# Sparse attention's first part laid out anew: keys by pairs of tiles, an order written out by hand, search steps spread differently

## The chip, the cores and the metric

The kernel runs on one core of one Trainium2 chip. The metric is device microseconds of one launch, taken as the median of several runs. Five engines work beside each other, each with its own queue of instructions: PE (TensorE, matmuls and transposes), DVE (VectorE), ACT (ScalarE), POOL (GpSimd) and SP, which here only issues transfers. An engine works through its queue strictly in order. PEld, where it appears, is the loading of weights on PE.

## The reference, cut to what matters

The program computes a two-layer decoder trunk on 1024 rows of 1024 numbers, in float32: sparse attention, a dense part, a gated recurrence and a second dense part. The change touches the attention alone, and of it what comes ahead of the softmax. In the reference that is:

```
h = x @ w_in
c_q, k, v, k_idx, w_idx = jnp.split(h, [256, 384, 512, 640], axis=-1)
c_q = rms_norm(c_q, g_cq)
q = (c_q @ w_uq)          # 16 heads of 64
q_idx = (c_q @ w_iq)      # 8 index heads of 128
k_idx = layer_norm(k_idx, g_ik, b_ik)
q, k, q_idx, k_idx = rope of each
score = einsum(w_idx, relu(q_idx . k_idx)), causal
_, sel = lax.top_k(score, 256)
out = softmax over the selected keys only, then @ w_o
```

Each query keeps the 256 keys with the highest score. The first 256 rows (tiles 0 and 1 of eight tiles of 128 rows) have no more than 256 causal keys, so they need no score.

## The kernel before, in words

**Tiles.** The rows are worked on as eight tiles of 128. Numbers with full float32 accuracy are made by three products of a high and a low part (`mm3`, lines 103 to 105), so a matmul of the source is three on PE, and `split` or `part` (lines 209, 210, 1186, 1187) makes the two parts, one on ACT and one on DVE.

**The first part, `att_in` (line 1150).** For each tile t there are five steps.
- `feature(t)` (line 1189) turns the tile of x by eight transposes on PE and splits it.
- `project(t)` (line 1214) multiplies it with `w_in`: 48 matmuls, 24 with 384 columns and 24 with 264.
- `keys(t)` (line 1233) makes what later tiles look at: on DVE it takes 33 instructions, among them the reciprocal root `rsqrt` (lines 111 to 116, eleven short instructions in a chain), two applications of `rope` (lines 202 to 205, four each), the norm's scaling (1255 to 1258), copies of keys out of PSUM (1269) and the low parts (1253, 210). PE makes seven transposes.
- `query(t)` (line 1282) makes the queries and the index queries, 12 matmuls of 512 columns each (24 in all), and POOL applies `rope` to both.
- `store(t)` (line 1305) turns them on PE in halves of eight transposes and writes them to DRAM. Of tiles 0 and 1 only the queries are written; their index queries are computed and never read.

**Scores and search.** `index(j)` (line 1356) makes the scores of tile j in units. A unit is three matmuls, a Relu on ACT (1383) and one instruction on DVE that adds the weighted result to the scores (1388). Tiles 2 and 3 have 8 units each, tiles 4 to 7 have 16 each, 80 in all. When the last unit of a tile is done, POOL masks its last 128 columns (1391). `search(js)` (line 1408) then finds the 256th highest score of two tiles at a time, bit by bit: twice 16 steps, each with a count on ACT (1436) for one tile and on DVE (1437) for the other, and two short instructions on DVE (1442, 1444) that set the next bound. With the steps ahead, between and behind it has 48 steps for each of the pairs (2, 3), (4, 5) and (6, 7). It ends with the mask of allowed keys, `bias` (1487).

**The second part, `att_main` (line 1491).** For each tile j there are 16 heads: logits on PE (1688), mask and minimum on DVE (1690), Exp on ACT (1692), transposes (1659), a copy on ACT (1661), products with the values (1664), and every eight heads `heads_out` (1694). The output projection (`att_out`) follows some heads later. Beside the heads of tile 1, POOL makes low parts of `w_o` (1505).

**What sets the order.** The program lists instructions in the order in which the Python code runs, and the framework then gives each engine a fixed queue; an instruction listed later may be put ahead of one that would wait. Scores and search are generators: `advance(i)` takes `STEPS[i]` = (units, steps) of them at four or five points of round i in `att_in`, and `att_main` takes `PLAN[j]` = (units, steps) behind each head of tile j. A generator that has to wait (for a tile that isn't stored, or for a buffer of scores that is still searched) gives its turn back without work. Worked out from these tables, the first part before takes 78 of the 80 units and 62 of the 144 search steps, the heads of tiles 0 and 1 take 2 units and 20 steps, and the heads of tiles 2 to 5 the other 62 steps. Round i of the first part lists `project(i)`, `store(i-2)`, `feature(i+1)`, `query(i-1)` and `keys(i)`:

```
        for i in range(NT + 2):
            if i < NT:
                project(i)
...
            if i >= 2:
                store(i - 2)
            advance(i)
            if i + 1 < NT:
                feature(i + 1)
            if 1 <= i <= NT:
                query(i - 1)
```

Transfers are all issued by SP, in order: the loads of x, the writes of `store` (1318), the loads of index queries (1366) and of queries (1585).

## Time and profile before

| what | value |
|---|---|
| median of 3 runs | 2638.32 us (2635.59 to 2641.08) |
| the profiled execution's own time | 2633.86 us |
| its span | 2632.1 us |
| PE busy | 2515.4 us, 96% |
| DVE busy | 2013.9 us, 77% |
| ACT busy | 1129.7 us, 43% |
| POOL busy | 250.0 us, 9% |
| mean granted clock of TensorE | 0.978 of full speed |

The table is of the whole span, in which attention takes about the first 700 us and the dense parts and the recurrence the rest. A share of busy time over the whole span therefore says little about the stretch that the change touches, and the stretches are read one by one below. Times inside the profile count from the span's start. Matmuls overlap in the pipeline, so the time between two starts is what a matmul costs, not its own length.

### The profile page before, as it was taken

The page shows a single profiled execution, that of the slowest core. Times are in us where ns is not written, and L with a number is a line of the kernel's source. Part 1 is how long each engine was busy: PE and PEld are TensorE (multiplying, and loading weights), DVE is VectorE, ACT ScalarE, POOL GpSimd, SP SyncE. Part 2 cuts the span into 40 slices and gives each one's busy share as a digit, 9 for nine tenths or more (in the row PEclk, how much of TensorE's full clock was granted, in tenths as well). Part 3 has the DMA queues.
Part 4 walks back from the last instruction along what each step waited for, and adds up shares of the span by engine and source line. Part 5 has one row for each costly group of instructions (what it writes and reads, how often), then busy time and mean ns, then how long its engine had stood idle before and what let it go on. Part 6 is the DMA issues. An engine that isn't in the chain of part 4 may idle for free.

```text
span 2632.1 us, 36939 instructions
## 1 busy us (share of the span) xinstructions
PE 2515.4 (96%) x13102; PEld 2090.3 (79%) x13102; DVE 2013.9 (77%) x4042; ACT 1129.7 (43%) x2176; POOL 250.0 (9%) x334
## 2 busy tenths in 40 slices
PE   8976799999999999999999999999899999999998
PEld 7764678888888788878788888888678888888786
DVE  6599899787778776656778888887786887665667
ACT  4576667665533233343544333333344323333431
POOL 1323421210000000000002111111000000000000
PEclk9998799999999999999999999999899999999999
DMA  3213200100366643385531111112535673336853
GB/s 134 91 48 126 87 23 21 53 30 8 106 232 233 234 160 119 95 281 187 197 104 52 61 53 53 41 69 77 190 115 180 233 243 103 113 91 223 275 176 128
DMA packets 156832, 332.06 MB, mean 126 GB/s; under 512 B 16368, under 2 KB 44776, under 8 KB 148968
## 3 DMA queue, kind: packets, MB, share of 16 engines
q1 hardware_dynamic: 156648, 329.71, 37.2%
q8 instruction: 103, 1.69, 0.3%
q14 instruction: 81, 0.66, 0.1%
HBM read 230.50 MB, written 99.09 MB: 125 GB/s over the span
## 4 chain that ended last, share of the span: by engine, by line
PE 62%; DVE 12%; DMA 8%; issue 3%; ACT 2%; SPq 1%; POOL 0%; DVEq 0%; ACTq 0%; POOLq 0%
PE M L105 9%; PE M L103 9%; PE M L104 9%; PE Y L103 6%; PE Y L104 6%; PE Y L105 6%; DMA wdt<-in_wd_dram 3%; PE Y L1023 3%; DMA t4q<-wdt 2%; DVE w L445 2%; PE O L1664 2%; PE L L1688 2%; PE Y L326 2%; DVE wdt L554 1%; PE O L1635 1%
## 5 line engine op out<-in xcount | busy, mean ns | idle before, releaser
L444 ACT CAST w<-raw 128x512 fp32r<-128x512 f32 (+1 forms) x373 | 289.2, 776 | 503.7 <-PE M L105 268.0
L445 DVE TENSOR_TENSOR w<-raw,w 128x512 fp32r<-128x512 f32 (+1 forms) x373 | 328.4, 883 | 175.7 <-ACT w L444 173.9
L103 PE MATMUL M<-x,w 128*128 128x512 f32 (+1 forms) x1120 | 434.1, 388 | 2.2 <-DVE e L478 2.1
L104 PE MATMUL M<-x,w 128*128 128x512 f32 (+1 forms) x1120 | 431.1, 385 | 0.0
L105 PE MATMUL M<-x,w 128*128 128x512 f32 (+1 forms) x1120 | 428.2, 382 | 3.0 <-DVE w L445 3.0
L105 PE MATMUL Y<-x,w 128*128 128x512 f32 (+1 forms) x644 | 244.8, 380 | 2.1 <-DVE w L445 2.1
L103 PE MATMUL Y<-x,w 128*128 128x512 f32 (+1 forms) x644 | 244.8, 380 | 1.2 <-DVE e L478 0.6
L105 PEld LDWEIGHTS M<-x,w 128*128 128x128 f32 x1120 | 212.4, 190 | 42.0 <-DVE w L445 3.2
L104 PE MATMUL Y<-x,w 128*128 128x512 f32 (+1 forms) x644 | 244.7, 380 | 0.0
L103 PEld LDWEIGHTS M<-x,w 128*128 128x128 f32 x1120 | 212.6, 190 | 40.4 <-DVE e L478 2.6
L104 PEld LDWEIGHTS M<-x,w 128*128 128x128 f32 x1120 | 212.7, 190 | 36.9 <-DVE w L445 0.2
L444 ACT CAST w<-s 128x512 fp32r<-128x512 f32 x180 | 112.0, 622 | 298.3 <-PE M L105 101.1
L445 DVE TENSOR_TENSOR w<-s,w 128x512 fp32r<-128x512 f32 x180 | 124.5, 692 | 42.2 <-ACT w L444 41.7
L105 PEld LDWEIGHTS Y<-x,w 128*128 128x128 f32 x644 | 121.1, 188 | 25.3 <-DVE w L445 2.5
L103 PEld LDWEIGHTS Y<-x,w 128*128 128x128 f32 x644 | 121.1, 188 | 24.8 <-DVE e L478 1.0
L104 PEld LDWEIGHTS Y<-x,w 128*128 128x128 f32 x644 | 121.1, 188 | 23.0
L1688 PE MATMUL L<-ks,qt 128*128 128x512 f32 (+5 forms) x384 | 114.4, 387 | 20.0 <-DVE nm L1690 16.8
L554 DVE TENSOR_TENSOR wdt<-wdt 128x512 f32<-128x512 f32 x104 | 71.8, 691 | 66.5 <-DMA wdt<-in_wd_dram 47.7
L103 PE MATMUL M<-w 128*128 128x512 f32 x288 | 113.6, 398 | 6.5 <-DVE rows L744 4.7
L104 PE MATMUL M<-w,w 128*128 128x512 f32 x288 | 113.5, 394 | 0.2 <-DVE w L445 0.2
L105 PE MATMUL M<-w,w 128*128 128x512 f32 x288 | 113.6, 395 | 0.0
L1692 ACT ACTIVATE p<-p,nm 128x128 f32<-128x128 f32 (+7 forms) x120 | 90.8, 757 | 38.2 <-DVE nm L1690 35.6
(471 smaller groups left out, 5585.4 us busy)
## 6 DMA issues: line engine op xcount, KB each, us to landing
raw<-in_wgu_dram SPq DMA_DIRECT2D x44, 1024.0 KB
wdt<-in_wd_dram SPq DMA_DIRECT2D x44, 512.0 KB
raw<-in_wd_dram SPq DMA_DIRECT2D x66, 256.0 KB
raw<-in_hw_dram SPq DMA_DIRECT2D x16, 1024.0 KB
qr<-qd SPq DMA_DIRECT2D x64, 128.0 KB
t5q<-wdt SPq DMA_DIRECT2D x26, 256.0 KB
t7q<-wdt SPq DMA_DIRECT2D x26, 256.0 KB
h7q<-s SPq DMA_DIRECT2D x26, 256.0 KB
```

What stands on the lines that cost most here:

```text
L103: mm(out, a[0], b[0], start=first, stop=False, **kw)
L104: mm(out, a[0], b[1], start=False, stop=False, **kw)
L105: mm(out, a[1], b[0], start=False, stop=last, **kw)
L326: mm(y[:, c], x[:, c], self.ident, **flags)
L444: self.nc.scalar.copy(hi, x)
L445: (eng or self.nc.vector).tensor_tensor(lo, x, hi.bitcast(F32), op=ALU.subtract)
L554: sub = lambda o, a, b: v.tensor_tensor(o, a, b, op=ALU.subtract)
L1023: nc.tensor.matmul(pl[rows, n, cols], lhs, rhs, start=True, stop=True)
L1635: nc.tensor.matmul(o, s.vhl[k0 + k][:, gi, :], y, start=first, stop=last)
L1664: nc.tensor.matmul(po[:, h * 64 : (h + 1) * 64], pT[:, i * P : (i + 1) * P], s.vv[:, k, gi * 64 : (gi + 1) * 64], start=k == 0, stop=k == j,)
L1688: nc.tensor.matmul(ps, s.qt[:, h % 4, :], s.ks[gi][i][:, kr], start=i == 0, stop=i == 1)
L1692: nc.scalar.activation(p, p, AF.Exp, bias=nm, scale=-1.0, accum_out=sm[:, h : h + 1])
```

## The change

Five things are changed, all in the attention.
- `att_in` follows a written order, `ORDER_IN`: p is project, f feature, k keys, q query, s store, w the loading of the query weights, a one call of `advance`. Four tiles are projected ahead of any query; the first queries are those of tiles 2 and 3, then come 0 and 1.
- `keys(p)` works on a pair of tiles: most of its instructions cover two tiles at once, which makes 37 instructions on DVE for a pair in place of 66. Its squares go into the buffer `kk`.
- `query(t)` leaves out the index queries of tiles 0 and 1: 12 matmuls, two copies on ACT and four instructions on POOL for each.
- The rope tables hold cos and sin twice side by side and once more in a short form, made by six more copies on POOL; `rope` takes them whole.
- `STEPS` and `PLAN` are new. Worked out from them, the first part takes 50 units and 52 search steps, the heads of tiles 0 and 1 take 30 units and 17 steps, and those of tiles 2 to 5 take 75 steps. x is loaded two tiles ahead by `feature`.

```diff
@@ -186,23 +183,28 @@
...
+            o, e = (self.tile(cp, [P, NT, 2, n], F32, f"rope{i}{n}") for n in (16, 8))
+            w = w.rearrange("p (t j) -> p t j", t=NT)
+            nc.scalar.activation(o[:, :, 0, :], w, AF.Sin, scale=2.0 * math.pi)
+            nc.gpsimd.tensor_copy(o[:, :, 1, :], o[:, :, 0, :])
+            for j in range(2):
+                nc.gpsimd.tensor_copy(e[:, :, j, :], o[:, :, 0, 0:16:2])
+            tabs.append((o, e))
+        return zip(*tabs)
+
...
-    def rope(self, eng, pool, tag, x, half, cos, sin):
...
+    def rope(self, eng, pool, tag, x, tabs):
...
@@ -1143,8 +1145,11 @@
                 self.att_main(bp, x, g, b)
 
 
-    STEPS = [(0, 0)] * 4 + [(1, 0), (4, 2), (6, 4), (5, 4), (6, 4), (6, 3)]
-    PLAN = [(1, 0.6), (1, 0.7), (0.4, 1.2), (0, 0.8), (0, 1.2), (0, 1.3), (0, 0), (0, 0)]
+    ORDER_IN = """p0 f2 p1 f3 k0 w p2 f4 p3 f5 k1 p4 f6 q2 s2 p5 f7 q3 s3 a q0 s0 a q1 s1 a k2 a
+        p6 a q4 s4 a p7 a q5 s5 a k3 a a q6 s6 a q7 s7 a a"""
+    STEPS = [(2, 0), (4, 0), (4, 0), (4, 0), (4, 3), (3, 5), (4, 6), (4, 6), (4, 7), (4, 7), (5, 7), (5, 6), (5, 5)]
+
+    PLAN = [(1, 0.5), (1, 0.6), (0.4, 1.1), (0, 1.0), (0, 1.4), (0, 1.4), (0, 0), (0, 0)]
     LATE = [10, 3, 3, 6, 8, 5, 11]
 
...
             xs[t] = (h, l)
-
-        feature(0)
+            if t + 2 < NT:
+                load_x(t + 2)
+
+        for t in range(2):
+            feature(t)
         for k in range(KD):
             part(wh[:, k, :], wl[:, k, :], win[k])
-        cos, sin = self.rope_tables(csp, tp, pos, inv)
+        wide, short = self.rope_tables(csp, tp, pos, inv)
         hs, cqt = {}, {}
 
         def query_weights():
...
                         k == 0,
                         k == KD - 1,
                     )
-            hc = self.tile(tp, [P, 520], F32, "hc", bufs=2)
+            if t % 2 == 0:
+                hs[t // 2] = self.tile(tp, [P, 2, 520], F32, "hc", bufs=2)
+            hc = hs[t // 2][:, t % 2, :]
             nc.scalar.copy(hc[:, 0:384], ps[0][:, 0:384])
             nc.scalar.copy(hc[:, 384:520], ps[1][:, 128:264])
             nc.scalar.copy(s.vv[:, t, :], ps[1][:, 0:128])
-            hs[t] = hc
-
-        def keys(t):
-
-            sl = slice(t * P, (t + 1) * P)
-            hc = hs.pop(t)
-            cq, kt, kin, wx = hc[:, 0:256], hc[:, 256:384], hc[:, 384:512], hc[:, 512:520]
-            v.tensor_scalar(s.wi[:, t, :], wx, 8**-0.5 * 128**-0.5, None, op0=ALU.mult)
-            sq = self.tile(tp, [P, 2], F32, "sq", bufs=2)
-            cqn = self.tile(tp, [P, 256], F32, "cqn")
-            nc.scalar.activation(cqn, cq, AF.Square, accum_out=sq[:, 0:1])
-            st = self.tile(tp, [P, 6], F32, "kist")
-            mv = self.tile(tp, [P, 2], F32, "kimv")
-            v.bn_stats(st, kin)
-            v.bn_aggr(mv, st)
-            v.tensor_scalar(sq[:, 0:1], sq[:, 0:1], 1.0 / 256, RMS_EPS - LN_EPS, op0=ALU.mult, op1=ALU.add)
-            v.tensor_copy(sq[:, 1:2], mv[:, 1:2])
-            k4 = kt.rearrange("p (g d) -> p g d", g=2)
-            self.rope(v, tp, "rk", k4[:, :, 0:16], 8, cos[:, t, 0:16:2], sin[:, t, 0:16:2])
-            kk = self.tile(tp, [P, 2, 2, 2, 64], F32, "kk")
+
+        def keys(p):
+
+            ts, sl = slice(2 * p, 2 * p + 2), slice(2 * p * P, (2 * p + 2) * P)
+            hc = hs.pop(p)
+            cq, kt, kin, wx = hc[:, :, 0:256], hc[:, :, 256:384], hc[:, :, 384:512], hc[:, :, 512:520]
+            v.tensor_scalar(s.wi[:, ts, :], wx, 8**-0.5 * 128**-0.5, None, op0=ALU.mult)
+            sq = self.tile(tp, [P, 2, 2], F32, "sq", bufs=2)
+            kk = self.tile(tp, [P, 2, 2, 2, 2, 64], F32, "kk")
+            junk = kk.rearrange("p i t g r d -> p (i t g r d)")[:, :256]
+            st = self.tile(tp, [P, 2, 6], F32, "kist")
+            mv = self.tile(tp, [P, 2, 2], F32, "kimv")
+            for t in range(2):
+                nc.scalar.activation(junk, cq[:, t, :], AF.Square, accum_out=sq[:, 0, t : t + 1])
+                v.bn_stats(st[:, t, :], kin[:, t, :])
+                v.bn_aggr(mv[:, t, :], st[:, t, :])
+            v.tensor_scalar(sq[:, 0, :], sq[:, 0, :], 1.0 / 256, RMS_EPS - LN_EPS, op0=ALU.mult, op1=ALU.add)
+            v.tensor_copy(sq[:, 1, :], mv[:, :, 1])
+            k4 = kt.rearrange("p t (g d) -> p t g d", g=2)
+            tabs = [x[:, ts].rearrange("p t (o j) h -> p t o (j h)", o=1).to_broadcast([P, 2, 2, 16]) for x in short]
+            self.rope(v, tp, "rk", k4[:, :, :, 0:16], tabs)
             for r in range(2):
-                nc.scalar.copy(kk[:, :, 0, r, :].bitcast(F32R), k4)
-                (gp if r else v).tensor_tensor(kk[:, :, 1, r, :], k4, kk[:, :, 0, r, :], op=ALU.subtract)
-            rs = self.rsqrt(sq, 2, 1.0, LN_EPS, "ai")
-            v.scalar_tensor_tensor(cqn, cq, rs[:, 0:1], gcq, op0=ALU.mult, op1=ALU.mult)
-            v.tensor_scalar(kin, kin, mv[:, 0:1], rs[:, 1:2], op0=ALU.subtract, op1=ALU.mult)
-            v.tensor_tensor(kin, kin, gik, op=ALU.mult)
-            v.tensor_tensor(kin, kin, bik, op=ALU.add)
-            self.rope(v, tp, "rk", kin[:, 0:32].rearrange("p (o d) -> p o d", o=1), 16, cos[:, t, :], sin[:, t, :])
-            pk = self.ps_c().rearrange("p (g j c) -> p g j c", g=2, j=2)
-            for i in range(2):
+                nc.scalar.copy(kk[:, 0, :, :, r].bitcast(F32R), k4)
+                (gp if r else v).tensor_tensor(kk[:, 1, :, :, r], k4, kk[:, 0, :, :, r], op=ALU.subtract)
+            rs = self.rsqrt(sq.rearrange("p a t -> p (a t)"), 4, 1.0, LN_EPS, "ai")
+            for t in range(2):
+                v.scalar_tensor_tensor(cq[:, t, :], cq[:, t, :], rs[:, t : t + 1], gcq, op0=ALU.mult, op1=ALU.mult)
+                x = kin[:, t, :]
+                v.tensor_scalar(x, x, mv[:, t, 0:1], rs[:, 2 + t : 3 + t], op0=ALU.subtract, op1=ALU.mult)
+            both = lambda x: x.rearrange("p (o d) -> p o d", o=1).to_broadcast([P, 2, P])
+            v.tensor_tensor(kin, kin, both(gik), op=ALU.mult)
+            v.tensor_tensor(kin, kin, both(bik), op=ALU.add)
+            self.rope(v, tp, "rk", kin[:, :, 0:32], [x[:, ts].rearrange("p t j h -> p t (j h)") for x in wide])
+            for g in range(2):
+                pk = self.ps_c().rearrange("p (j t c) -> p j t c", j=2, t=2)
                 for j in range(2):
-                    nc.tensor.transpose(pk[:, i, j, :], kk[:, i, j].rearrange("p r d -> p (r d)"), self.ident)
-            for i in range(2):
+                    for t in range(2):
+                        nc.tensor.transpose(pk[:, j, t, :], kk[:, j, t, g].rearrange("p r d -> p (r d)"), self.ident)
                 for j in range(2):
-                    if i == 0:
-                        nc.scalar.copy(s.ks[i][j][:, sl], pk[:, i, j, :])
-                    else:
-                        v.tensor_copy(s.ks[i][j][:, sl], pk[:, i, j, :])
+                    x = pk[:, j].rearrange("p t c -> p (t c)")
+                    (v.tensor_copy if g else nc.scalar.copy)(s.ks[g][j][:, sl], x)
             pc = self.ps_c()
             for i in range(2):
-                nc.tensor.transpose(pc[:, i * P : (i + 1) * P], cqn[:, i * P : (i + 1) * P], self.ident)
-            nc.tensor.transpose(pc[:, 256:384], kin, self.ident)
-            h = self.tile(tp, [P, 2, P], F32R, "cqh", bufs=4)
-            l = self.tile(tp, [P, 2, P], F32R, "cql", bufs=4)
-            self.split(h, l, pc[:, 0:256].rearrange("p (k c) -> p k c", k=2))
-            self.split(s.kih[:, sl], s.kil[:, sl], pc[:, 256:384])
-            cqt[t] = (h, l)
+                for t in range(2):
+                    c = (2 * i + t) * P
+                    nc.tensor.transpose(pc[:, c : c + P], cq[:, t, i * P : (i + 1) * P], self.ident)
+            pi = self.ps_c()[:, :256]
+            for t in range(2):
+                nc.tensor.transpose(pi[:, t * P : (t + 1) * P], kin[:, t, :], self.ident)
+            h, l = (self.tile(tp, [P, 2, 2, P], F32R, f"cq{x}", bufs=2) for x in "hl")
+            self.split(h, l, pc.rearrange("p (k t c) -> p k t c", k=2, t=2))
+            self.split(s.kih[:, sl], s.kil[:, sl], pi)
+            cqt[p] = (h, l)
 
         qs = {}
...
 
-            h, l = cqt.pop(t)
-            c8, s8 = cos[:, t, 0:16:2], sin[:, t, 0:16:2]
+            h, l = (x[:, :, t % 2, :] for x in cqt[t // 2])
             q = self.tile(tp, [P, 16, 64], F32, "q")
             qi = self.tile(tp, [P, 8, P], F32, "qi")
-            for w, d in ((wq, q), (wk, qi)):
+            todo = [(wq, q, 16, short), (wk, qi, 32, wide)][: 1 if t < 2 else 2]
+            for w, d, m, tabs in todo:
                 ps = self.ps_a()
                 for c in range(2):
                     for k in range(2):
@@ -1298,8 +1313,9 @@
                         )
                     dv = d.rearrange("p (c n) d -> p c (n d)", c=2)[:, c, :]
                     nc.scalar.activation(dv, ps[c], AF.Copy, scale=-0.125 if w is wq else 1.0)
-            self.rope(gp, tp, "rq", q[:, :, 0:16], 8, c8, s8)
-            self.rope(gp, tp, "rq", qi[:, :, 0:32], 16, cos[:, t, :], sin[:, t, :])
+            for w, d, m, tabs in todo:
+                tabs = [x[:, t : t + 1].rearrange("p o j h -> p o (j h)").to_broadcast([P, d.shape[1], m]) for x in tabs]
+                self.rope(gp, tp, "rq", d[:, :, :m], tabs)
             qs[t] = (q, qi)
 
...
                 nc.sync.dma_start(dst, y)
                 if t < 2:
                     break
-            s.stored = t
-
-        def advance(i):
-            for gen, n in zip((s.index, s.find), self.STEPS[i]):
+            s.stored = max(s.stored, t)
+
+        s.idx_ps = self.ps_c
+        s.index, s.find, s.stored = self.indexes(), self.searches(), -1
+        steps = iter(self.STEPS)
+
+        def advance():
+            for gen, n in zip((s.index, s.find), next(steps)):
                 for _ in range(n):
                     next(gen, None)
 
-        s.idx_ps = self.ps_c
-        s.index, s.find, s.stored = self.indexes(), self.searches(), -1
-        for i in range(NT + 2):
-            if i < NT:
-                project(i)
-                if i + 2 < NT:
-                    load_x(i + 2)
-            if i > 4:
-                advance(i)
-            if i >= 2:
-                store(i - 2)
-            advance(i)
-            if i + 1 < NT:
-                feature(i + 1)
-            if 1 <= i <= NT:
-                query(i - 1)
-            advance(i)
-            if i < NT:
-                keys(i)
-            if i == 0:
-                query_weights()
-            advance(i)
+        does = dict(p=project, f=feature, k=keys, q=query, s=store, w=lambda _: query_weights(), a=lambda _: advance())
+        for step in self.ORDER_IN.split():
+            does[step[0]](int(step[1:] or 0))
 
```

## Rows read from the trace of the kernel before

**Rows 1.** Busy time by stretch: stretch, length, PE, PEld, DVE, ACT, POOL, clock, DMA.
```profile
0.00:43.00 43.00, 30.89 (x157) 26.65 (x158) 32.51 (x111) 22.39 (x44) 4.86 (x14) 0.96 0.51 180
43.00:132.00 89.00, 83.75 (x503) 73.70 (x502) 48.55 (x165) 47.46 (x119) 31.48 (x52) 1.00 0.25 80
132.00:219.00 87.00, 65.13 (x323) 51.85 (x321) 82.89 (x269) 57.55 (x155) 28.85 (x44) 0.91 0.19 61
219.00:254.00 35.00, 24.62 (x79) 16.58 (x79) 34.30 (x79) 25.47 (x53) 10.42 (x10) 0.84 0.52 175
254.00:321.00 67.00, 50.49 (x246) 41.19 (x246) 58.05 (x157) 46.55 (x139) 32.52 (x22) 0.72 0.25 79
321.00:407.00 86.00, 81.78 (x504) 69.05 (x502) 78.94 (x193) 57.69 (x135) 20.13 (x23) 0.96 0.09 26
407.00:518.00 111.00, 106.52 (x748) 96.23 (x747) 90.77 (x260) 78.44 (x172) 23.48 (x29) 0.97 0.12 39
```

**Rows 2.** POOL in order of time: start, length; line 1391 masks scores, 1487 writes a bias.
```profile
131.72 0.29 POOL L1391 TENSOR_SCALAR_AFFINE_SELECT sc<-sc 128x128 f32<-128x128 f32 x1 [1.36 <-DVE sc L1388]
...
219.42 0.91 POOL L1487 TENSOR_SCALAR bias<-high 128x512 bf16<-128x512 f16 x1 [1.57 <-DVE high L1486]
```

**Rows 3.** PE in order of time at full clock: the steps of the first part.
```profile
42.42 0.60 PE L1263 MATMUL C<-ident,kk 128*128 128x128 f32 x4
...
43.11 0.42 PE L103 MATMUL A<-winh,xsh 128*128 128x384 f32 x1
...
50.32 1.03 PE L1316 MATMUL B<-ident,q 128*128 128x128 f32 x8
...
51.98 0.47 PE L103 MATMUL A<-w_uqh,cqh 128*128 128x512 f32 x1
...
57.32 0.39 PE L105 MATMUL A<-w_iqh,cql 128*128 128x512 f32 x1
```

**Rows 4.** PE in order of time, early: waits are in brackets.
```profile
6.81 1.94 PE L1197 MATMUL C<-ident,xin 128*128 128x128 f32 x8 [6.81 <-DMA xin<-in_x_dram]
...
33.35 0.66 PE L1197 MATMUL C<-ident,xin 128*128 128x128 f32 x4 [1.42 <-DVE xsl L210]
```

**Rows 5.** Instruction groups on DVE, 0 to 205 us: count, then busy us, mean ns.
```profile
L114 DVE TENSOR_TENSOR ait<-aiy 128x2 f32<-128x2 f32 x24 | 4.7, 194 | 0.4
L202 DVE TENSOR_TENSOR rk<-hc,rope 128x32 f32<-128x32 f32 x16 | 4.5, 282 | 11.4 <-ACT hc L1228 11.1
L210 DVE TENSOR_TENSOR cql<-C,cqh 128x256 fp32r<-128x256 f32 x8 | 3.3, 416 | 0.0
L204 DVE TENSOR_TENSOR hc<-hc,rk 128x16 f32<-128x16 f32 x16 | 3.1, 192 | 0.3
L210 DVE TENSOR_TENSOR kil<-C,kih 128x128 fp32r<-128x128 f32 x8 | 2.3, 289 | 1.7 <-ACT kih L209 1.7
L112 DVE TENSOR_SCALAR aiy<-aih 128x2 int32<-128x2 int32 x8 | 1.3, 166 | 0.2
```

**Rows 6.** Instruction groups on DVE, 132 to 219 us.
```profile
L114 DVE TENSOR_TENSOR ait<-aiy 128x2 f32<-128x2 f32 x6 | 1.8, 302 | 0.1
L1460 DVE TENSOR_TENSOR low<-low,bias 128x512 uint16<-128x512 uint16 x1 | 0.4, 425 | 0.0
```

**Rows 7.** Instruction groups on DVE, 0 to 330 us.
```profile
L1437 DVE TENSOR_SCALAR_CACHE_REDUCE low<-high,clow 128x768 uint16<-128x768 uint16 x16 | 16.1, 1008 | 0.4
L1388 DVE SCALAR_TENSOR_TENSOR sc<-rel,wi,sc 128x512 f32<-128x512 f32 x21 | 15.3, 750 | 7.9 <-ACT rel L1383 7.7
```

**Rows 8.** Instruction groups on DVE, 321 to 518 us: the last search.
```profile
L1437 DVE TENSOR_SCALAR_CACHE_REDUCE high<-low,clow 128x1024 uint16<-128x1024 uint16 x16 | 20.5, 1279 | 0.3
L1444 DVE SCALAR_TENSOR_TENSOR clow<-clow,rej 128x2 f32<-128x2 f32 x37 | 9.9, 268 | 0.5
L1442 DVE TENSOR_SCALAR rej<-cnt 128x2 f32<-128x2 f32 x37 | 7.8, 210 | 1.1 <-ACT low L1436 0.7
```

**Rows 9.** Instruction groups on POOL, 0 to 330 us.
```profile
L203 POOL TENSOR_TENSOR qi<-qi,rope 128x256 f32<-128x256 f32 x8 | 5.9, 739 | 0.6
```

**Rows 10.** DVE in order of time, beside POOL's work for the weights.
```profile
280.77 2.58 DVE L1460 TENSOR_TENSOR low<-low,bias 128x768 uint16<-128x768 uint16 x1
...
303.49 2.27 DVE L1444 SCALAR_TENSOR_TENSOR clow<-clow,rej 128x2 f32<-128x2 f32 x1
```

**Rows 11.** POOL in order of time at the same place.
```profile
277.56 5.38 POOL L1505 TENSOR_TENSOR xl<-resid,xh 128x1024 fp32r<-128x1024 f32 x2
```

More of the change, by code (lines that the diff above doesn't have):

```diff
@@ L155, in rope_tables @@
         v.tensor_copy(pf, pt)
-        ang = self.tile(wp, [P, NT, 16], F32, "ang")
+        three = self.tile(wp, [P, 3, n], F32, "kk")
+        ang, a1, a2 = (three[:, i, :] for i in range(3))
         v.tensor_tensor(
-            ang,
+            ang.rearrange("p (t j) -> p t j", t=NT),
             pf.rearrange("p (t o) -> p t o", o=1).to_broadcast([P, NT, 16]),
@@ L162, in rope_tables @@
         )
-        ang = ang.rearrange("p t j -> p (t j)")
-        a1 = self.tile(wp, [P, n], F32R, "ang1")
-        v.tensor_copy(a1, ang)
-        a2 = self.tile(wp, [P, n], F32, "ang2")
-        v.tensor_tensor(a2, ang, a1.bitcast(F32), op=ALU.subtract)
-        a1 = a1.bitcast(F32)
+        v.tensor_copy(a1.bitcast(F32R), ang)
+        v.tensor_tensor(a2, ang, a1, op=ALU.subtract)
         turns = self.tile(wp, [P, 7, n], F32, "q")
@@ L188, in rope_tables @@
             v.tensor_scalar(w, w, -0.4999999, 0.4999999, op0=ALU.max, op1=ALU.min)
-            o = self.tile(cp, [P, NT, 16], F32, f"rope{i}")
-            nc.scalar.activation(o.rearrange("p t j -> p (t j)"), w, AF.Sin, scale=2.0 * math.pi)
-            tabs.append(o)
-        return tabs
-    def rope(self, eng, pool, tag, x, half, cos, sin):
-        nh = x.shape[1]
-        shape = [P, nh, 2, half]
-        xv = x.rearrange("p n (j h) -> p n j h", j=2)
-        bc = lambda a: a.rearrange("p (o u h) -> p o u h", o=1, u=1).to_broadcast(shape)
-        tmp = self.tile(pool, [P, nh * 2 * half], F32, tag)
-        tmp = tmp.rearrange("p (n j h) -> p n j h", n=nh, j=2)
-        eng.tensor_tensor(tmp, xv, bc(sin), op=ALU.mult)
-        eng.tensor_tensor(xv, xv, bc(cos), op=ALU.mult)
-        eng.tensor_tensor(xv[:, :, 0, :], xv[:, :, 0, :], tmp[:, :, 1, :], op=ALU.subtract)
-        eng.tensor_tensor(xv[:, :, 1, :], xv[:, :, 1, :], tmp[:, :, 0, :], op=ALU.add)
+            o, e = (self.tile(cp, [P, NT, 2, n], F32, f"rope{i}{n}") for n in (16, 8))
[7 more added lines that the diff above has]
+    def rope(self, eng, pool, tag, x, tabs):
+        cos, sin = tabs
+        n = math.prod(x.shape[1:])
+        names = " ".join("abc"[: len(x.shape) - 1])
+        dims = dict(zip("abc", x.shape[1:]))
+        tmp = self.tile(pool, [P, n], F32, tag).rearrange(f"p ({names}) -> p {names}", **dims)
+        h = x.shape[-1] // 2
+        eng.tensor_tensor(tmp, x, sin, op=ALU.mult)
+        eng.tensor_tensor(x, x, cos, op=ALU.mult)
+        lo, hi = (..., slice(0, h)), (..., slice(h, 2 * h))
+        eng.tensor_tensor(x[lo], x[lo], tmp[hi], op=ALU.subtract)
+        eng.tensor_tensor(x[hi], x[hi], tmp[lo], op=ALU.add)
     def split(self, hi, lo, x):
```

## The prediction, made before the changed kernel ran

> **What bounds it now.** I read the busy time by stretch first, then the timelines of PE and POOL in the first part, then the groups on DVE. The reader is to see four stretches [rows 1]. From 43 to 132 us PE is busy 83.8 of 89 us at full clock while DVE works 48.6: PE bounds. From 132 to 254 us it is the reverse: DVE is busy 82.9 of 87 and 34.3 of 35, PE 65.1 and 24.6. This is the search of tiles 2 and 3, the scores of tiles 4 to 7 and the last keys. From 254 to 321 us, the heads of tiles 0 and 1, nothing is full: DVE 58.1 of 67, PE 50.5 at a granted clock of 0.72. From 321 to 518 us both are nearly full: PE 188.3 of 197, DVE 169.7. So the kernel loses time because DVE is half idle early (89 - 48.6 = 40.4 us) and overloaded later. What counts is when DVE's long work can begin, and how much there is. It begins when the scores of tile 3 are masked, at 131.7 us, and its first search ends at 219.4 us [rows 2].
>
> **Part A, up to the scores of tile 3: -14 us.** Prices on PE at full clock, from start to start [rows 3]: keys of a tile 43.11 - 42.42 = 0.7; project 50.32 - 43.11 = 7.2; one half of a store and one feature together 1.66, so 0.83 each; a query of 24 matmuls 57.32 - 51.98 plus one gap of 0.23 = 5.6. Listed ahead of the last unit of tile 3 before: 6 project 43.3, 5 query 27.9, 6 keys 4.1, 7 features 5.8, 6 halves of stores 5.0, in sum 86.1. After: 6 project 43.3, two queries 11.1 and two without index queries 5.6, 6 keys 4.1, 8 features 6.6, 6 halves 5.0, in sum 75.7. The 16 units are the same in both. That is -10.4. Before, PE also idles 43.0 - 30.9 = 12.1 us up to 43 us [rows 1]; 6.8 of it is the wait for x [rows 4], which stays. The other 5.3 contain waits such as the 1.42 us at 33.35, where DVE is late while the first tile's keys and query stand next in line; after, projects 2 and 3 stand there. I take 3.6 of the 5.3. Bounds: nothing, if the fixed queues had already filled these gaps, up to -20, half of DVE's idle 40.4.
>
> Moved and added work, priced at nothing here. The two stores and query steps of tiles 0 and 1 go behind those of 2 and 3, with their transfers on SP's queue; the loads of index queries for tile 2 now follow two stores in place of one, and project 5 (7.2 us) and query 3 cover their way through DRAM. Without that cover the scores start some us later, inside the bound of nothing. The six table copies on POOL cost under 0.74 us each by the nearest row, a 256-column product [rows 9], so at most 4.4 us and surely above nothing; projects 2 and 3 hide them, and if they didn't, the first pair's keys would be that much later. POOL loses eight such instructions. Loading x by `feature` moves an issue on SP only. Where keys wait for a pair, tile 0's keys wait for tile 1; no one reads them before the queries.
>
> **Part B, keys by pairs: -6 us.** A pair takes 37 instructions on DVE in place of 66. The reciprocal root's five groups sum to 16.3 us (first and last: 4.7 and 1.3), rope's four to 14.4 (4.5 and 3.1) [rows 5]. Halving the root gives -8.2. Halving rope gives -7.2; each remaining instruction is 16 to 32 columns longer, and 128 columns cost 0.416 - 0.289 = 0.127 us, so at most +1.0. The other 40 instructions that go save their fixed part, 0.289 - 0.127 = 0.16 us each, -6.4. In sum -20.8 us for four pairs. Three pairs lie in the stretch where DVE has idle time and save nothing on the path. The keys of tiles 6 and 7 lie in the full stretch (6 of 24 calls of line 114), a quarter, -5.2, and there a call costs 0.302 in place of 0.194 us [rows 5, 6]. I take -6, bounds -4 to -8.
>
> **Part C, 219 to 321 us: -9 us.** By the tables, 28 units move from the first part to the heads of tiles 0 and 1. Most were made at 214 to 262 us anyway, so this is an order of the same work. But up to the end of tile 1's heads the second search has 21 steps in place of 34: 13 steps of about 1.01 + 0.27 + 0.21 = 1.49 us leave, -19 of DVE's 92.4 us [rows 1, 7, 8]. If DVE bounds alone, all of it comes back; if the heads' own chain bounds (DVE has 9 us idle in 254 to 321), nothing. I take half.
> What speaks against it: beside the heads of tile 1, DVE instructions on SBUF take far longer while POOL works. An operation of 512 columns takes 0.425 us alone; with 768 columns, at 280.77, it takes 2.58 while POOL makes low parts of weights, and an instruction on two numbers takes 2.27 [rows 6, 10, 11]. The 28 moved instructions of 0.75 us [rows 7] now stand in that place. 768 columns alone would be some 0.425 x 1.5 = 0.64 us, so 1.94 are lost; at half of that on each unit, C would be -9 + 28 x 0.97 = +18. I keep -9, since such POOL work covers only a part of the two stages.
> The Trainium skill says of this (SBUF — State Buffer, "Who interferes with whom") that a DVE instruction with two SBUF inputs is fully blocked by a GpSimd instruction that reads SBUF, and the row of 2.58 us agrees; by that rule alone every moved unit that meets POOL waits it out, which is the rival R2 below.
>
> **Part D, 321 to 518 us: +5 us.** The 13 steps come back here, beside the last search, at 1.28 + 0.27 + 0.21 = 1.76 us: +23 on DVE's 169.7, in 197 us [rows 1, 8]. The fullest long stretch that the trace shows is 82.9 of 87, or 95%; (169.7 + 23) / 0.953 = 202, so +5. Bounds: 0 if heads leave room, +23 if none of it fits.
>
> **Sum.** -14 - 6 - 9 + 5 = -24 us. Against the profiled execution's own 2633.9 us that is 2609.9. This execution is 4.4 us under the median of the runs, 2638.3, below the lowest of them; on the median the forecast is 2614 us. What a measurement of this kernel can tell from no change is about 0.2%, 5.3 us.
>
> **Rivals.**
> R1, the order isn't kept. The queues are laid by the framework, and instructions listed later already fill gaps. Then only removed work counts: A falls to -5.6 (24 matmuls of 0.23 us), B -6, C 0, D +5: -6.6, 2632 us. Against it: 40 us of DVE idle are there, so the gaps aren't filled. 0.14.
> R2, POOL's block eats the gain. C is +18 in place of -9: -14 - 6 + 18 + 5 = +3, 2641 us. For it, the 2.58 us; against it, POOL is busy only 32.5 of 67 us there. 0.11.
> R3, slower: the search that was put off becomes the wait of 321 to 518 us. Of DVE's 27 idle us, 20 lie from 407 to 518 us [rows 1], where little search is left before; now 8 more steps fall in tile 5's heads. DVE's queue is in order, so the heads' minimum stands behind counts of 1.28 us and PE waits for it. It decides from the point where the added 23 us exceed what the heads leave, some 7 us in 321 to 407. Then D is +23, C nothing, and PE loses clock as it does at 0.72 in 254 to 321; I price that at 8 us, from 188 us of PE's work at 0.96 against 0.92. -14 - 6 + 23 + 8 = +11, 2649 us. 0.09.
> R4, more: DVE bounds all through 132 to 321 us, A is -20, B -6, C -19, D 0 to +5: -40 to -45, 2596 us. 0.20.
> The forecast, 2604 to 2625 us: 0.46.
>
> **Numbers.** The likeliest is 2614 us. The range 2594 to 2640 takes in R1, R2 and most of R4 and leaves out R3 and the far end of R4. Faster by over 0.2%, below 2633 us: the forecast, R4 and most of R1, 0.76. Within 0.2%: the rest of R1 and most of R2, 0.13. Slower by more: R3 and a little of R2, 0.11.
>
> **What would show it.** Right: the mask of tile 3's scores near 114 to 118 us, not 131.7; the bias of tile 3 near 196 to 202, not 219.4; DVE's sum up to 518 us smaller by 21; heads of tile 6 starting some 24 us earlier; from there on the same spacing to the end. A is wrong if tile 3's mask stays beyond 125 us, B if line 114 isn't at 12 calls with about half its time, C if the heads of tiles 0 and 1 together take over 80 us, D if PE is under 93% busy beside the last two searches. The whole is wrong if PE in the second part waits for DVE's minimum longer than it does now.

## The result: 15 us faster, and the profile after

The changed kernel takes 2623.3 us (median of 4 runs, 2620.9 to 2628.2) where the kernel before takes 2638.6 (4 runs beside it): a ratio of 0.9943, with a 95% interval of 0.9928 to 0.9958. The forecast was 2614; faster was right, by 15 us in place of 24.

A stage is read here from one first event to the next: the mask of tile 3's scores, the first minimum of tile 2's heads, that of tile 6's, and the last minimum of all. Busy time by these stages, before (the stretches up to the mask are nearly those of [rows 1]); columns as there:

```profile
131.72:322.80 191.08, 142.32 (x660) 111.36 (x659) 177.20 (x509) 131.40 (x352) 72.08 (x76) 0.83 0.27 88
322.80:523.80 201.00, 192.30 (x1274) 168.87 (x1273) 171.44 (x456) 137.81 (x306) 45.50 (x52) 0.97 0.10 32
523.80:637.00 113.20, 111.13 (x701) 92.26 (x700) 91.89 (x224) 72.40 (x134) 11.45 (x12) 1.00 0.08 24
```

The same stages of the changed kernel:

```profile
0.00:43.00 43.00, 32.35 (x199) 30.09 (x200) 32.17 (x89) 22.04 (x44) 3.20 (x15) 1.00 0.58 192
43.00:123.31 80.31, 72.55 (x420) 63.78 (x420) 38.55 (x101) 40.39 (x92) 23.71 (x35) 0.96 0.21 66
123.31:308.80 185.49, 142.94 (x675) 115.53 (x674) 160.81 (x429) 121.52 (x325) 78.42 (x84) 0.82 0.30 97
308.80:505.10 196.30, 185.79 (x1260) 161.75 (x1258) 185.23 (x504) 147.25 (x332) 41.35 (x43) 0.99 0.10 33
505.10:621.20 116.10, 114.08 (x712) 95.75 (x712) 92.42 (x226) 72.50 (x136) 15.30 (x22) 0.98 0.08 24
```

The mask comes 8.4 us earlier (123.3 for 131.7), the next stage is 5.6 shorter, the one after 4.7 shorter, the last 2.9 longer: 15.8 us at the last minimum. DVE lost 16.4 us of work in the second stage (177.2 to 160.8), of which the stage gave back only a third: DVE was busy 93% of it and is now busy 87%.

The events on POOL that answer to [rows 2]:

```profile
123.31 0.30 POOL L1392 TENSOR_SCALAR_AFFINE_SELECT sc<-sc 128x128 f32<-128x128 f32 x1 [7.97 <-DVE sc L1389]
...
211.76 0.66 POOL L1488 TENSOR_SCALAR bias<-high 128x512 bf16<-128x512 f16 x1
```

Both miss their marks: the mask was to be at 114 to 118, tile 3's bias at 196 to 202. What PE waited for between 43 and 123 us (us in total, times, longest):

```profile
PE B L1332 <- POOL q L207: 5.4, 4, 2.2
PE B L1332 <- POOL qi L207: 2.2, 2, 1.3
```

Before, the same two waits of `store` for POOL's rope, from 43 us to the mask, came to 0.6 and 1.6 us:

```profile
PE B L1316 <- POOL qi L205: 1.6, 1, 1.6
...
PE B L1316 <- POOL q L205: 0.6, 1, 0.6
```

Now each store stands right behind its query in the written order, with POOL's rope between them and nothing else listed there for PE.

Groups on DVE, 0 to 205 us, that answer to [rows 5]: pairs more than halved them.

```profile
L114 DVE TENSOR_TENSOR ait<-aiy 128x4 f32<-128x4 f32 x12 | 1.9, 161 | 0.3
L203 DVE TENSOR_TENSOR rk<-hc,rope 128x64 f32<-128x64 f32 x8 | 1.9, 239 | 13.7 <-ACT hc L1238 13.6
```

### The profile page after: what moved, and what is told of

It is laid out like the page before. It is cut to its first block, busy times and chain, and to the rows that moved or that the text cites. A ratio compares the mean times of both kernels' runs of the same rounds, so it can differ in the third digit from the quotient of the medians.

```text
span 2619.1 us, 36693 instructions
## 1 busy us (share of the span) xinstructions
PE 2503.0 (96%) x13078; PEld 2083.3 (80%) x13078; DVE 2001.8 (76%) x3926; ACT 1120.7 (43%) x2148; POOL 247.0 (9%) x328
## 4 chain that ended last, share of the span: by engine, by line
PE 66%; DVE 12%; DMA 5%; issue 3%; ACT 2%; SPq 1%; DVEq 0%; ACTq 0%
PE M L104 9%; PE M L105 9%; PE M L103 9%; PE Y L103 7%; PE Y L104 7%; PE Y L105 7%; PE Y L1025 2%; DMA wdt<-in_wd_dram 2%; PE Y L328 2%; PE L L1689 2%; PE O L1665 1%; DVE w L447 1%; DMA t4q<-wdt 1%; PE O L1636 1%; DVE p L1691 1%
## 5 line engine op out<-in xcount | busy, mean ns | idle before, releaser
L1689 PE MATMUL L<-ks,qt 128*128 128x512 f32 (+5 forms) x384 | 113.4, 383 | 20.8 <-DVE nm L1691 16.5
L1665 PEld LDWEIGHTS O<-vv,pT 128*128 128x128 f32 x672 | 91.2, 199 | 14.7 <-ACT pT L1662 10.6
```

What stands on the lines that cost most here:

```text
L1665: nc.tensor.matmul(po[:, h * 64 : (h + 1) * 64], pT[:, i * P : (i + 1) * P], s.vv[:, k, gi * 64 : (gi + 1) * 64], start=k == 0, stop=k == j,)
L1689: nc.tensor.matmul(ps, s.qt[:, h % 4, :], s.ks[gi][i][:, kr], start=i == 0, stop=i == 1)
```

## Experiments

Each is an edit of the changed kernel unless it says otherwise. The table collects them; ratios are to the kernel before, run beside each; the events are those above, in us.

| run | ratio, 95% interval | mask of 3 | heads of 2 | heads of 6 | last minimum |
|---|---|---|---|---|---|
| before | 1 | 131.7 | 322.8 | 523.8 | 637.0 |
| changed | 0.9943, 0.9928 to 0.9958 | 123.3 | 308.8 | 505.1 | 621.2 |
| changed, again | 0.9940, 0.9924 to 0.9955 | 122.3 | 307.4 | 503.8 | 618.4 |
| keys by tile | 0.9955, 0.9940 to 0.9970 | 125.4 | 307.8 | 504.2 | 621.4 |
| all index queries | 0.9919, 0.9901 to 0.9937 | 123.3 | 302.7 | 499.0 | 613.7 |
| old spread | 0.9979, 0.9966 to 0.9992 | 121.7 | 317.2 | 516.5 | 629.8 |
| stores apart | 0.9919, 0.9902 to 0.9937 | 124.8 | 301.7 | 498.1 | 612.4 |
| low parts on DVE | 0.9876, 0.9860 to 0.9892 | 122.1 | 290.0 | 487.2 | 601.6 |
| rope on DVE | 0.9912, 0.9899 to 0.9926 | 113.3 | 292.0 | 488.3 | 601.8 |
| stores covered | 0.9920, 0.9908 to 0.9933 | 119.5 | 301.3 | 497.7 | 612.3 |
| before, low parts on DVE | 0.9952, 0.9939 to 0.9965 | 131.2 | 310.9 | 506.1 | 619.3 |
| low parts, keys by tile | 0.9905, 0.9892 to 0.9919 | 123.3 | 293.5 | 490.0 | 604.6 |
| low parts and rope | 0.9847, 0.9834 to 0.9861 | 114.3 | 284.6 | 481.1 | 598.0 |
| all three | 0.9854, 0.9840 to 0.9867 | 114.6 | 282.0 | 478.6 | 593.3 |

**The changed kernel again.** No edit.

> The changed kernel itself, unaltered, beside the next three on the same chip. What differs from its first profile is what a profile of one and the same program can differ by: if a stretch's time is fixed by the program, the mask of tile 3's scores comes at 123.3 and the last minimum of the heads at 621.2 within 0.5 us; if not, differences of a few us between the other runs of these stages prove nothing.

The mask moved by 1.0 us and the last minimum by 2.8 (1.5 of them in the last stage), so neither repeats within 0.5 us, while single runs lay between 2614 and 2627 us. Differences of up to 3 us at the last minimum say nothing below. Where "the second profile" is named, it is the one of this run.

**Keys tile by tile.**

```
-        def keys(p):
...
+        def keys(p):
+            both = hs.pop(p)
...
+            for i in range(2):
+                key(2 * p + i, both[:, i, :], h[:, :, i, :], l[:, :, i, :])
```

> The changed kernel (2623.3 us) with one part undone: keys are made tile by tile again (33 instructions on DVE for a tile, as before), everything else stays. Forecast's view (part B: only the last pair's keys lie on the path): about 6 us slower, 2629. First rival (keys save nothing on the path, since DVE had room all along): within 2 us of 2623. Second rival (DVE is the limit from the first projects to the second pair of heads, and each pair's keys stand ahead of the queries that wait for them): most of the 20.8 us come back, 2635 or more, no faster than the kernel before.

2627.2 us, a ratio 0.0012 to 0.0015 above the changed kernel's, 3 to 4 us, and 0.2 to 3.0 at the last minimum. The heads of tile 0 begin at 218.9 us in place of 198.2, yet those of tile 1 at 250.7 where they began at 251.2: twenty us of earlier heads didn't bring the next ones forward. The second rival, 2635 or more, falls; between the first and the forecast this run can't tell.

**Index queries of tiles 0 and 1 made again.**

```
-            todo = [(wq, q, 16, short), (wk, qi, 32, wide)][: 1 if t < 2 else 2]
+            todo = [(wq, q, 16, short), (wk, qi, 32, wide)]
```

> The changed kernel with the index queries of tiles 0 and 1 computed again (24 matmuls on PE, 5.5 us at 0.23 us each, four copies on ACT, eight instructions on POOL). If PE's listed work sets the end of the first scores: the mask of tile 3's scores moves from 123.3 to about 129 us and the whole takes about 2627 to 2629. If POOL's rope is what the first scores wait for, POOL's eight instructions (four of about 0.74, four of about 0.45 us) stand in the way besides and the mask comes later than 130. If PE has room there: mask within 2 us of 123.3, the whole within 2 us of 2623.

The mask doesn't move. Busy time by stretch, changed kernel, then this one:

```profile
90.00:110.00 20.00, 15.94 (x72) 13.47 (x71) 6.79 (x12) 11.09 (x24) 8.81 (x14) 0.83 0.31 101
```

```profile
90.00:110.00 20.00, 18.15 (x95) 14.50 (x94) 5.86 (x10) 11.68 (x25) 12.56 (x20) 1.00 0.29 89
```

The extra matmuls stand in PE's waits for POOL, and the granted clock rises from 0.83 to 1.00. Leaving this work out was worth nothing. With it the kernel is, if anything, faster: the ratio is lower, with overlapping intervals, and the last minimum comes 4.7 us earlier than in the second profile, all of it between the mask and the heads of tile 2. From 150 to 170 us the granted clock is 1.00 here and 0.83 in both profiles of the changed kernel; whether that is the cause isn't shown, and no expectation covers it.

**Old spread of units and steps.**

```
-    STEPS = [(2, 0), (4, 0), (4, 0), (4, 0), (4, 3), (3, 5), (4, 6), (4, 6), (4, 7), (4, 7), (5, 7), (5, 6), (5, 5)]
...
-    PLAN = [(1, 0.5), (1, 0.6), (0.4, 1.1), (0, 1.0), (0, 1.4), (0, 1.4), (0, 0), (0, 0)]
+    STEPS = [(2, 0), (4, 0), (4, 0), (4, 0), (4, 3), (8, 8), (8, 8), (8, 8), (8, 8), (0, 8), (10, 8), (10, 6), (10, 5)]
...
+    PLAN = [(1, 0.6), (1, 0.7), (0.4, 1.2), (0, 0.8), (0, 1.2), (0, 1.3), (0, 0), (0, 0)]
```

> The changed kernel with units and search steps spread as before the change: 78 units and 62 steps in the first part, the heads of tiles 2 to 5 take 62 steps in place of 75, and the old shares per head. Order, keys by pairs and the missing index queries stay. Forecast's view (parts C and D together -4): 2627. Rival one (the spread is worth nothing, an order of the same work): 2621 to 2625. Rival two (the spread is the main gain, since without it DVE is full up to the heads of tile 2): 2632 or more. In the profile the heads of tiles 0 and 1 start later than the 198 us of the changed kernel and take less time; the heads of tile 2 start within 5 us of 308.8 by the forecast, 10 or more later by rival two.

2634.1 us, in the range of rival two; but the heads of tile 2 come 8.4 us later, between the marks of the forecast (5) and of rival two (10), and DVE isn't full ahead of them. Order, pairs and left-out queries alone make 0.2%; the spread makes the rest, 8.6 us at the last minimum (11.4 against the second profile). The stages of this run:

```profile
121.72:317.20 195.48, 150.24 (x671) 118.48 (x670) 167.84 (x478) 133.59 (x350) 79.64 (x84) 0.79 0.28 93
317.20:516.50 199.30, 190.62 (x1273) 167.25 (x1272) 171.34 (x456) 137.68 (x306) 45.46 (x52) 0.97 0.10 32
```

The first is 4.4 us longer than before although DVE has 9.4 us less to do, and it is busy 86% of it: 4.4 of the 10.0 us gained at the mask are given back there. PE's waits in it, then before's in its own stage:

```profile
PE C L103 <- ACT it L1369: 10.2, 6, 7.0
PE B L1332 <- POOL qi L207: 7.8, 4, 2.4
...
PE L L1689 <- DVE nm L1691: 4.5, 8, 1.1
PE B L1332 <- POOL q L207: 4.3, 3, 2.4
PE C L103 <- ACT rel L1384: 4.0, 6, 1.4
```

```profile
PE C L103 <- ACT rel L1383: 18.5, 16, 3.1
PE L L1688 <- DVE nm L1690: 13.5, 13, 2.8
...
PE B L1316 <- POOL q L205: 1.5, 1, 1.5
...
PE C L103 <- ACT it L1368: 0.8, 2, 0.6
```

Waits for rope and for the split index queries (`it`) grew; before, PE waited longer for Relu (`rel`) and for the heads' minimum (`nm`). In sum PE idles less than before, 45.2 us for 48.8, so these rows alone don't show what made the stage longer.

**Stores apart, and stores covered.** Two other orders in the first part, each shown up to the end of the line. In the first one tiles 0 and 1 are ahead of 2 and 3 again.

```
+    ORDER_IN = """p0 f2 p1 f3 k0 w p2 q0 f4 p3 s0 q1 f5 k1 p4 s1 q2 f6 p5 s2 q3 f7 a s3 a a k2 a
...
```

> The changed kernel with another written order in the first part: each query is followed by a project or a query before its store (p2 q0 f4 p3 s0 q1 f5 k1 p4 s1 q2 f6 p5 s2 q3 f7 a s3 a a k2 a p6), so that POOL's rope has time; the same work is listed ahead of the last unit of tile 3. If the waits of PE for POOL's rope (0.84, 1.26, 2.21 and 1.85 us between 83 and 105 us) and the clock lost in them are what ate the early gain: the mask of tile 3's scores comes at 116 to 118 us in place of 123.3, the whole at 2616 to 2619. If these waits only took the place of others: mask within 2 us of 123.3, whole within 2 us of 2623. If the gain is made but given back at DVE's later work: mask at 116 to 118 and the whole at 2622 to 2625.

```
+    ORDER_IN = """p0 f2 p1 f3 k0 w p2 f4 p3 f5 k1 p4 f6 q2 p5 f7 s2 q3 a p6 s3 a q0 a k2 s0 q1 a s1
...
```

> The changed kernel with a written order in which another project or query stands between each query and its store, with tiles 2 and 3 still first (q2 p5 f7 s2 q3 a p6 s3 a q0 a k2 s0 q1 a s1 a q4). All PE work ahead of the last unit of tile 3 is the same. If PE is the limit once its waits are covered: the mask of tile 3's scores at 115 to 118 us and the whole at 2612 to 2618. If the units' own way (loads of index queries through DRAM, Relu on ACT, the sum on DVE) is the limit: mask within 2 us of 123.3, whole 2617 to 2623.

Both gain some 6 us (by the ratios, whose intervals overlap the changed kernel's, and at the last minimum against the second profile, beyond its 3 us), but the mask stays at 124.8 in the one and falls only to 119.5 in the other. Up to the mask PE's waits for POOL's rope, 7.6 us in the changed kernel, are gone in the first and 3.4 in the second. The first pays for it in another way: it turns the index queries of tile 2 at 82.8 us in place of 69.5, and PE's first unit comes at 92.3 in place of 85.0. So these waits alone don't set the mask, against my expectation, and an order that covers them helps at the end all the same.

**Rope of tiles 0 to 3 on DVE.**

```
-                self.rope(gp, tp, "rq", d[:, :, :m], tabs)
+                self.rope(v if t < 4 else gp, tp, "rq", d[:, :, :m], tabs)
```

> The changed kernel with rope of the queries of tiles 0 to 3 on DVE in place of POOL; DVE is half idle there. If PE's waits for POOL's rope set the first scores: these waits (0.84, 1.26, 2.21, 1.85 us) fall below 0.5 each, the granted clock of 90 to 110 us goes from 0.83 to 1, and the mask of tile 3's scores comes at 117 to 119 us in place of 123.3. If the index queries' way (store, DRAM, load, split) sets them: mask within 2 us of 123.3 with the waits gone all the same.

The mask comes at 113.3, below the expected range, and PE is full where it waited (one wait for rope is left, 1.4 us):

```profile
90.00:110.00 20.00, 19.64 (x116) 16.84 (x117) 11.97 (x24) 13.19 (x30) 4.36 (x6) 1.00 0.28 79
```

Up to the mask PE idles 11.3 us, where it idles 16.7 in the second profile. So POOL's rope is what holds up the first scores in this order. The whole gains 7 us by the ratios (0.9940 to 0.9912); the execution profiled was the fastest of its five by 9 us, so its later events may flatter it.

**Low parts of the output weights on DVE.**

```
-            gp.tensor_tensor(l, r, h.bitcast(F32), op=ALU.subtract)
+            v.tensor_tensor(l, r, h.bitcast(F32), op=ALU.subtract)
```

> The changed kernel with the eight low parts of the output weights made on DVE in place of POOL (2.3 to 3.0 us each on POOL). If POOL's block is what the heads of tile 1 lose their time to (score units of 0.74 us take 1.55 to 1.84 us beside it, a two-number instruction 2.27, and PE waits 4.0 us for a low part): the heads of tile 1 fall from 57.6 to about 48 to 52 us and the whole comes at 2615 to 2619. If DVE's own sum is the limit there: eight more instructions of about 1.3 us on DVE, 10 us, make the heads of tiles 0 and 1 as long as now or up to 10 us longer, 2623 to 2633.

2603.4 us beside 2618.2 for the changed kernel. That is the first theory, with about twice its size: 2615 to 2619 was expected, and the heads of tile 1 take 42.6 us where 48 to 52 were. Groups, 190 to 325 us, of the changed kernel's second profile, on POOL and then on DVE:

```profile
L1506 POOL TENSOR_TENSOR xl<-resid,xh 128x1024 fp32r<-128x1024 f32 x8 | 20.0, 2500 | 5.3 <-ACT xh L1505 3.6 <-PE T L1660 1.0 <-PE I L105 0.5
```

```profile
L1389 DVE SCALAR_TENSOR_TENSOR sc<-rel,wi,sc 128x512 f32<-128x512 f32 x14 | 13.4, 954 | 3.1 <-ACT rel L1384 3.0
```

The same groups of this run, both on DVE:

```profile
L1389 DVE SCALAR_TENSOR_TENSOR sc<-rel,wi,sc 128x512 f32<-128x512 f32 x14 | 11.4, 820 | 0.4 <-ACT rel L1384 0.4
...
L1506 DVE TENSOR_TENSOR xl<-resid,xh 128x1024 fp32r<-128x1024 f32 x8 | 10.0, 1248 | 0.0
```

The stage up to the heads of tile 2, in the second profile and in this run:

```profile
122.28:307.40 185.12, 142.19 (x675) 115.43 (x674) 160.55 (x427) 121.45 (x325) 78.97 (x84) 0.82 0.30 97
```

```profile
122.14:290.00 167.86, 136.18 (x666) 110.01 (x664) 155.56 (x431) 120.59 (x323) 59.39 (x76) 0.86 0.33 107
```

DVE took on 10.0 us of work and was still busy 5 us less than the 160.6 of the second profile, since its other instructions stretch less. The stage is 17.3 us shorter. PE's wait of 4.0 us for a low part is gone, its waits for DVE's minimum fall from 12.8 to 7.8 us, and DVE is now busy 93%. How the 17 us divide among these isn't told apart.

**The kernel before with low parts on DVE** (the same edit, at its line 1505).

> The kernel before the change, with the eight low parts of the output weights made on DVE in place of POOL. If POOL's block became dear only through the change, because the 30 units that were moved into the heads of tiles 0 and 1 now stand beside it: the old kernel gains little, 0 to 5 us (2633 to 2638), where the changed one gained 15. If the block cost the old kernel as much (its DVE instructions of 2.27 and 2.58 us): 10 to 16 us, 2622 to 2628, and the change did not make it worse.

2625.0 us, 13 faster, and 17.7 earlier at the last minimum, where the changed kernel gained 16.8. The second theory holds: POOL's block cost the old kernel nearly as much, and the change didn't make it dear.

**Low parts on DVE with keys tile by tile** (both edits above).

> The changed kernel with the low parts of the output weights on DVE and with keys made tile by tile. If pairs of keys are worth DVE time that only POOL's block hid: 8 us or more above the kernel with the low parts on DVE alone (2603), so 2611 or more, and the last minimum of the heads at 608 or later in place of 601.6. If the tile-by-tile keys lie in time that DVE has anyway, but for the last pair: 2 to 5 us above, 2605 to 2608.

2613.6 us, a ratio 0.0029 above the run with low parts alone, which is 8 us, but 3.0 at the last minimum. With POOL's block gone, pairs are worth 3 to 8 us; the two measures speak for one theory each, so the runs don't decide between them.

**Both edits, and with the covered order too.**

> The changed kernel with both edits: low parts of the output weights on DVE, and rope of the queries of tiles 0 to 3 on DVE. If the two losses lie one behind the other (first scores 9 us earlier, heads of tile 1 some 15 us shorter): the gains add, 2618 - 15 - 6 to -16, that is 2588 to 2597, with the mask of tile 3's scores near 113 and the last minimum near 586 to 592. If the second gain needs the slack that the first one uses: 2599 to 2604.

> The last one with the written order that puts another project or query between each query and its store. If PE's waits for POOL's rope still cost something once rope is on DVE: the mask of tile 3's scores 2 to 4 us earlier than in the kernel with both edits and the whole 2 to 4 us faster. If not: within 2 us of it, either way.

2598.6 and 2600.0 us: both beat both kernels, by 1.5% against before. The gains of low parts (17 us by ratios) and rope (7) come to 24 together against the changed kernel, so by the time they add, though the median falls just short of the expected range. The profile shows less: of the mask's 7.8 us over low parts alone, 5.4 are left at the heads of tile 2, 6.1 at those of tile 6 and 3.6 at the last minimum, where 10 or more were expected; the last stage alone takes from 113.5 to 117.2 us over runs of the changed kernel that leave it unaltered. The covered order doesn't move the mask, and adds 2.5 us at the heads of tile 6, 4.7 at the last minimum and nothing in the time, so "within 2 us" holds.

## Why the forecast was right in sign and short in size

The last minimum takes the sum apart: the old spread gives C and D with the last stage, keys by tile give B, the rest is A. The first figure is against the first profile of the changed kernel, the second against the second. That the terms add is taken for granted; A and B together are 7.2 us either way, from before to the old spread.

| term | forecast | measured |
|---|---|---|
| A, first scores | -14 | -8.4 to -9.4 at the mask; -7.0 or -4.2 at the end |
| B, pairs | -6 | -0.2 or -3.0; -3 to -8 by ratios |
| C and D, spread | -4 | -8.6 or -11.4 |
| sum | -24 | -15.8 or -18.6 |

**A is where it failed,** though its own mark, a mask beyond 125 us, wasn't reached. The work left out was sized about right: PE is busy 104.9 us up to the mask for 114.4, 9.5 less where 10.4 were forecast. The 3.6 us of idle time that were to go as well didn't: PE idles 18.4 us for 17.4. Up to 43 us it idles less, 10.7 for 12.1, though its wait for x grew from 6.8 to 8.1; from there to the mask it idles 7.8 for 5.3, and 7.6 of that is rope. The wrong step is the sentence that priced the moved stores and queries at nothing because "project 5 and query 3 cover their way through DRAM". It prices the way through DRAM and not what stands ahead of it, POOL's rope (eight instructions, four for tiles 0 and 1), which nothing covers when a store follows its query. Two runs bear it out: work put into these waits cost nothing, and rope on DVE moved the mask by 9 us. The first of the two other orders limits it: with these waits gone but tile 2's index queries stored later, the mask stays. So the 5.6 us for left-out index queries, counted in full even under R1, were worth nothing. I also counted six projects ahead of the last unit; the trace of either kernel has seven (56 of line 103's 384-column matmuls, eight a project), which leaves the difference alone. Halves of stores I counted as six in both; before there are eight (64 transposes of line 1316), so the list should have said some 12 us less and not 10.4. And the bound that tile 3's mask was to set wasn't one: with the old spread 4.4 of the 10.0 us gained there are lost again before the heads of tile 2, beside longer waits for rope and for the split index queries. That these waits are the cause isn't shown: before, PE idles even longer there, for other reasons. The two other orders, which gain 6 us, speak for it, but cover only tiles 0 to 3.

**B's size isn't settled.** By the last minimum pairs are worth at most 3.0 us, which is within what one kernel's profiles differ by and under the bounds of 4 to 8; by the ratios they are worth 3 to 4 us, and 8 with the low parts on DVE. The groups of line 114 and of rope's first line fell from 9.2 to 3.8 us, more than the half forecast, and most of what DVE saves doesn't reach the end, as forecast; that it is the last pair's share that does wasn't tried by itself.

**C was right in size, in part by luck, and its test was not.** From the old spread to the new one the stage up to the heads of tile 2 falls by 10.0 us (195.5 to 185.5); the forecast said 9, half of the 19 us that DVE was to lose. DVE lost only 7.0 (167.8 to 160.8), since its instructions got longer there (the units by some 7 us in sum, see R2 below), and the stage fell by more than that. Yet the heads of tiles 0 and 1 take 110.6 us, over the 80 that were to refute it; before, they took 94.7. They begin 30 us earlier (198.2 for 228.1) and so hold more: in the traces 40 units stand ahead of them in place of 59, with about the same search, and with the old spread alone they begin at 216.8, with keys by tile alone at 218.9. A stage's length isn't a test when its start moves; its end is.

**D was too high.** DVE's work there rose by 13.9 us (171.3 with the old spread to 185.2), not 23, though 12 of the 13 steps came (48 in place of 36 behind the first minimum of tile 2), and 185.2 of 196.3 is 94%, inside the 95% I had taken as full. PE is busy 94.6%, over the 93 that were to refute D, and its clock is 0.99 for 0.97. But the old kernel with low parts on DVE runs this part, in which it isn't altered, in 195.2 us in place of 201.0, and the changed one with that edit in 197.2:

```profile
310.90:506.10 195.20, 187.20 (x1278) 163.33 (x1278) 171.18 (x462) 139.86 (x311) 46.75 (x52) 1.00 0.10 33
```

```profile
290.00:487.20 197.20, 187.17 (x1269) 163.47 (x1268) 186.01 (x508) 147.98 (x332) 41.55 (x44) 0.99 0.10 33
```

So the new spread makes this part 3.0 us shorter with the low parts on POOL and, beside other changes, 2.0 longer without. The part's length varies by as much as D was to cost; of D it is shown that it cost less than 5, not its sign.

**The other signs.** DVE's sum up to 518 us was to be smaller by 21; it is the same (426.0 and 425.6), since 518 us now stands later in the work. Up to the heads of tile 6 it is 12.7 us smaller (429.5 to 416.8). Those heads start 18.7 us earlier, not 24. PE's wait for DVE's minimum, which was to refute the whole if it grew, came to 16.8 us before from the first minimum to the last, and to 16.5 and 17.1 in the two profiles of the changed kernel: it neither refutes nor supports anything.

**The rivals.** R1 fell (the mask moved by more than the left-out work). R2 took the right place for a change it doesn't belong to: moving the block was worth 13 to 17 us, but in both kernels. The tables' 28 units are 19 in the traces (from the first minimum of tile 0 to that of tile 2 DVE adds 21 units before and 40 after), and my price of 0.97 us each was about four times too high: from the old spread to the new one a 512-column unit goes from 0.763 to 0.954 us on the mean, one of 448 columns from 0.704 to 1.020 (190 to 325 us, second profile). R3 and R4 didn't come.

## What to carry to other kernels

In a written order, look for what each step hands to the next engine and how long that engine takes: a step put right behind the one that feeds it costs the bound engine its wait, and work left out of such a wait was worth nothing here. Before search steps are balanced around an engine that is nearly full, ask which of its instructions are long only because of a neighbour: moving eight instructions off POOL was worth as much as the whole change. And judge a stage by when it ends.

## What the runs showed of the hardware

**POOL's cost to DVE is more than the work it takes off it.** One low part takes 2.50 us on POOL and 1.25 on DVE. In DVE's order of time, changed kernel, beside a low part that POOL makes from 284.12 to 286.47:

```profile
280.14 0.16 DVE L1445 SCALAR_TENSOR_TENSOR clow<-clow,rej 128x2 f32<-128x2 f32 x1
...
283.49 0.70 DVE L1443 TENSOR_SCALAR rej<-cnt 128x2 f32<-128x2 f32 x1
284.22 2.27 DVE L1445 SCALAR_TENSOR_TENSOR clow<-clow,rej 128x2 f32<-128x2 f32 x1
286.52 1.01 DVE L1438 TENSOR_SCALAR_CACHE_REDUCE low<-high,clow 128x768 uint16<-128x768 uint16 x1
```

An instruction on two numbers lasts until POOL's ends; the same one at 280.14, between two of POOL's, takes 0.16. The Trainium skill says (SBUF — State Buffer, "Who interferes with whom") that the port pair which DVE shares with GpSimd is an exclusive lock, and that an instruction of DVE with two SBUF inputs contends with a GpSimd instruction that reads SBUF. The trace agrees, with 2.27 us beside 0.16. The Trainium skill also advises against elementwise work with two inputs on GpSimd, as about twice as slow (GPSIMD Engine Reference, "4.1 Engine selection"), and 2.50 against 1.25 agrees too.

**PE lost clock beside short waits.** No wait of PE between 43 and 123 us exceeded 2.21 us, yet the granted clock was 0.83 from 90 to 110 us: it fell to the lower of its two levels (1.2 GHz) for 3.4 us each from 96.1 and from 106.3 us, just behind waits for POOL's rope of 2.21 and 1.85 us. With 24 more matmuls ahead of them these waits are 0.61 and 1.24 us, the clock stays at 1.00 and the mask comes no later. It also stays at 1.00 in the run with stores covered, with a wait of 1.9 us, so which wait, or what sum of them, brings it down isn't shown.
